# Two-layer decoder trunk on one core: the small fp32 matmuls of the state space and of the attention heads are issued in longer runs, and the last heads' transposes come one stage later

## The chip, the cores and the metric

The kernel runs on one core of a Trainium2 chip. The metric is device time in microseconds (us); of the kernel before it is the median of three runs. A core has five engines with a program each: TensorE (PE, matrix products), VectorE (DVE), ScalarE (ACT), GpSimd (POOL) and SyncE (SP, which here only starts DMAs). They meet at semaphores.

## The reference

A trunk of two layers over 256 tokens of 2048 channels, all in fp32. Layer 0 mixes tokens with a state space (Mamba-2: 64 heads of 64 channels in 8 groups), layer 1 with a forgetting attention (16 heads of 128 channels). Each layer goes on with a SwiGLU feed-forward and a per-layer embedding. Cut to what the change touches:

```python
# state space, per group of 8 heads, in 2 chunks of 128 tokens
y = ssd_chunked_scan(xs, dt, a, bm, cm) + xs * d_skip
y = y * silu(z)
yg = y.reshape(b, l, g, SSD_D_INNER // g)
yg = yg * lax.rsqrt(jnp.mean(yg * yg, axis=-1, keepdims=True) + EPS)   # one mean per group and token
mix = (yg.reshape(b, l, SSD_D_INNER) * norm_w) @ w_out

# attention, per head and block of 128 queries
s = q[lo:hi] @ k[:hi].T + csum[lo:hi, None] - csum[None, :hi]          # masked above the diagonal
o = softmax(s) @ v[:hi]
```

## The kernel before

**The stream of weights.** Almost all the work is products of the 256 tokens with weights. SP streams the weights from HBM in blocks of 512 KB (`raw`). ACT casts a block to the reduced type fp32r (`wh`, line 182) and DVE subtracts to get the part that was lost (`wl`, line 187). Activations are kept in two parts as well. So a product of a 128 x 128 weight block is two matmuls on PE: `wh` with both parts of the activations, 512 columns (line 249), and `wl` with the high part, 256 columns (line 251). Both kinds are exact to fp32 together. A `unit` (line 202) takes a column block of the weights and runs through its rows in stages of one weight block each, into 4 PSUM accumulators `acc` (6 in the last units of a layer's part); the pool `psa` has six banks for them. PSUM's two other banks are the tile `mi` of `misc()` (line 272), for everything small.

**The tasks in between.** After each stage, `unit` takes a task from the queue `bg` (lines 254 to 256) and emits it. A `noop` in the queue moves what follows by a stage. So the order of the lists of tasks sets in which stage a small piece of work stands. A scheduler that walks through the program with modelled durations then puts the instructions of all engines in their final order; `joined` (line 312) tells it that the rest of a run of matmuls may be issued only after the first of them, so that the run comes in one piece where the scheduler sees its data ready. With `hold` the order of the program is kept as well, and the next stage follows the run.

**State space.** For a group g the tasks of `core_tasks` (line 946) compute the decays on ACT (`decay`, `decay2`), transpose the group's x (`xpose`, line 961) and multiply: `ymm` (line 1008) issues 16 fp32 matmuls whose outputs have 64 partitions. They come as eight pairs (s = 0, 1), the two of a pair on different halves of PE's columns; in four of the pairs each matmul has 256 columns, in the four others 128. `y_of` (line 1012) adds the skip term on DVE. The gate's unit (`z_unit`, line 1093) multiplies y by silu(z), squares it (`sumsq`, lines 297 to 301: ACT squares, DVE adds to the tile `gss`), and then come three tasks of `gate_tasks` (line 1028): `gn1` sums `gss` over its partitions with two matmuls of one column with `ones` (`rstd_small`, line 331) and takes the root on POOL, `gn2` spreads it (`rstd_wide`, line 347), `gn3` scales y. The tile `gss` has one buffer, so that the next group's first square waits until the sums are done.

**Attention.** The four quads of heads come from `quad_tasks` (line 1258): `scores` of two heads (four matmuls, line 1267, then DVE and the exponentials on ACT), `norm` (line 1287, a division on DVE), `turns` (six 128 x 128 transposes, line 1299, then two copies `pT` on ACT, line 1306) and `values` (eight matmuls, line 1315). The last quad stands under the output projection, whose stages are six accumulators wide and take 12 matmuls each; before that projection's column 12 the queue is drained (`need`, line 1348), which sets where the last `values` stand.

Of the kernel before, what the change touches and what calls it, by code (L numbers as in the profile page):

```python
# [7 lines left out]
F32 = mybir.dt.float32  # L8
# [6 lines left out]
P = 128  # L15
T = 256
# [5 lines left out]
NG = 8  # L22
# [34 lines left out]
def tile_trunk(ctx, tc, a, out):  # L57
# [214 lines left out]
    def misc():  # L272
        return psm.tile([P, 512], F32, tag="mi", name=nm("mi"))
# [51 lines left out]
        turn.append(last_v[0])  # L325
        return r

    def rstd_small(acc, n):
        ps = misc()
        for j in range(2):  # L330
            PE.matmul(ps[:, j:j + 1], lhsT=acc[:, j * P:(j + 1) * P], rhs=ones[:, :1],
                      start=True, stop=True)
        ms = tmp("ms", (P, 2))
        dmark[0] = V.tensor_scalar(out=ms, in0=ps[:, :2], scalar1=1.0 / n, scalar2=EPS,  # L334
                                   op0=mult, op1=add)
        rs = tmp("rs", (P, 2), bufs=3)
        G.tensor_tensor(out=rs, in0=ms, in1=mhalf, op=ALU.pow)  # L337
        return rs
# [464 lines left out]
    with ExitStack() as ys:  # L803
        yp = pool(ys, "yp", side="right")
        y = [yp.tile([P, T], F32, name=f"y{c}") for c in range(32)]
        with ExitStack() as st:
# [136 lines left out]

            s3 = [None]

            def core_tasks(g, xg):
                S = {}
                for q in range(2):
                    h0 = 8 * g + 4 * q
                    ab = s3[0].tile([P, 4, T], F32, tag="ab", name=nm("ab"), bufs=2)  # L950
                    G.dma_start(
                        out=ab.rearrange("p a n -> p (a n)"),
                        in_=acd[h0:h0 + 4, :].rearrange("h n -> (h n)").partition_broadcast(P))
                    S[f"a{q}"] = ab

# [51 lines left out]

                def ymm():
                    todo = ymm_of(1) + ymm_of(0)
                    joined(todo[0], todo[1:])  # L1010

                def y_of(q):
                    for pr in range(2):
# [6 lines left out]
                def ymm_y():  # L1020
                    ymm()
                    y_of(1)

                return [lambda: decay(0, 0), lambda: decay(0, 1), xpose, lambda: decay2(0),
                        lambda: decay(1, 0), lambda: decay(1, 1), lambda: decay2(1), noop, ymm_y,
                        lambda: y_of(0), noop]

            def gate_tasks(g, S):
                def gn1():
                    S["rs"] = rstd_small(S["ss"], 512)  # L1030

                def gn2():
                    S["rw"] = yp.tile([P, T], F32, tag="grw", name=nm("grw"), bufs=1)
                    rstd_wide(S["rs"], S["rw"])

                def gn3():
                    for c in range(4):
                        yc = y[4 * g + c]
                        last_v[0] = V.scalar_tensor_tensor(out=yc, in0=yc, scalar=col("ssd_norm", 4 * g + c),
                                               in1=S["rw"], op0=mult, op1=mult)  # L1040
                if g < NG - 2:
                    return [noop, gn1, gn2, gn3]
                late.append(lambda: paced(gn3))
                return [noop, gn1, gn2] if g < NG - 1 else [gn1, noop, gn2, noop]

# [45 lines left out]
            left = [0]  # L1091

            def z_unit(g, pops):
                S = {}

                def ev_z(t, acc):
                    if t == 0:
                        while len(bg) > left[0]:
                            bg.popleft()()
                    if t == 0:  # L1100
                        S["ss"] = yp.tile([P, T], F32, tag="gss", name=nm("gss"), bufs=1)
                        if g == 0:
                            gated(0, z00)
                    if g == 0:
                        t += 1
                    yc = y[4 * g + t]
                    if g == NG - 1:
                        later.append((acc, yc, S["ss"]))
                        return
                    z = tmp("g0")  # L1110
                    gather(acc, z)
                    gated(t, z)

                def gated(t, z):
                    yc = y[4 * g + t]
                    V.tensor_tensor(out=z, in0=z, in1=rwide2, op=mult)
                    th = tmp("th")
                    A.activation(th, z, AF.Tanh)
                    V.scalar_tensor_tensor(out=z, in0=th, scalar=1.0, in1=z, op0=add, op1=mult)
                    V.tensor_tensor(out=yc, in0=yc, in1=z, op=mult)  # L1120
                    sumsq(S["ss"], yc, t == 0)
                unit(lambda k: xs0[k], ev_z, pops=pops)
                if g < NG - 1:
                    bg.extend(gate_tasks(g, S))
                else:
                    last7.extend([late[0]] + gate_tasks(g, S) + [late[1]])
# [127 lines left out]
    ots = [newx() for _ in range(FH)]  # L1254

    RNG = ((0, P), (P, 384))

    def quad_tasks(hds, q, k):
        ck = load_ck(hds[0] // 4)
        S = [{} for _ in hds]  # L1260

        def scores(j0):
            pss = [misc(), misc()]

            def mm(i, b):
                qT, kT = q[j0 + i], k[j0 + i]
                return PE.matmul(pss[i][:, RNG[b][0]:RNG[b][1]], lhsT=qT[:, b * P:(b + 1) * P],  # L1267
                                 rhs=kT[:, :(b + 1) * P], start=True, stop=True)
            joined(lambda: mm(1, 0), [lambda i=i, b=b: mm(i, b)
                                      for i, b in ((1, 1), (0, 0), (0, 1))])  # L1270
            for i in (1, 0):
                hd, ps = hds[j0 + i], pss[i]
                sc = fp.tile([P, 384], F32, tag="sc", name=nm("sc"), bufs=4)
# [13 lines left out]
        def norm(j0):  # L1287
            for i in (1, 0):
                sc, sm = S[j0 + i]["sc"], S[j0 + i]["sm"]
                V.reciprocal(out=sm, in_=sm)  # L1290
                for j, (b, e) in enumerate(RNG):
                    V.tensor_scalar(out=sc[:, b:e], in0=sc[:, b:e], scalar1=sm[:, j:j + 1],
                                    scalar2=None, op0=mult)

        def turns(j0):
            pss = [misc(), misc()]

            def turned(i, b):
                return PE.transpose(out=pss[i][:, b * P:(b + 1) * P],
                                    in_=S[j0 + i]["sc"][:, b * P:(b + 1) * P], identity=ident)  # L1300
            joined(lambda: turned(0, 2), [lambda i=i, b=b: turned(i, b) for i in range(2)
                                          for b in range(3) if (i, b) != (0, 2)],
                   hds[-1] == FH - 1)
            for i in range(2):
                pT = fp.tile([P, 384], F32, tag="pT", name=nm("pT"), bufs=4)
                A.copy(out=pT, in_=pss[i][:, :384])
                S[j0 + i]["pT"] = pT

        def values():
            pss = [misc(), misc()]  # L1310

            def mm(i, b):
# [1 line left out]
                o = pss[i // 2][:, (i % 2) * T:(i % 2 + 1) * T]  # L1314
                return PE.matmul(o[:, b * P:], lhsT=vt[:, b, hd * P:(hd + 1) * P],  # L1315
                                 rhs=S[i]["pT"][:, b * T:(T, 384)[b]], start=b == 0, stop=b == 1)
            joined(lambda: mm(3, 0), [lambda i=i, b=b: mm(i, b)
                                      for i, b in ((3, 1), (2, 0), (2, 1), (1, 0), (1, 1), (0, 0), (0, 1))],
                   hds[-1] == FH - 1)
            for i in range(4):  # L1320
                split(pss[i // 2][:, (i % 2) * T:(i % 2 + 1) * T], ots[hds[i]])

        if hds[-1] == FH - 1:
            return [noop, lambda: scores(0), lambda: scores(2), lambda: norm(0), noop,
                    lambda: (turns(0), norm(2)), noop, lambda: turns(2), noop, values]
        return [noop, lambda: scores(0), noop, lambda: scores(2), lambda: norm(0), noop,
                lambda: (turns(0), norm(2)), noop, lambda: turns(2), noop, values]

    for u in range(4):
        q = [fp.tile([P, T], F32, tag="qk", name=nm("q"), bufs=12) for _ in range(4)]  # L1330
# [104 lines left out]
```

## Time and profile before

| what | value |
|---|---|
| time, median of 3 runs | 2753.42 us (2752.81 to 2754.73) |
| the profiled execution's own time | 2754.77 us |
| its span | 2753.0 us |
| PE busy | 2745.7 us |
| DVE busy | 1906.7 us |
| ACT busy | 1481.1 us |
| mean traffic from and to HBM | 188 GB/s |
| mean granted clock of PE | 1.0 |

The span is the time from the first to the last instruction of the profiled execution; 1.8 us of its own time lie around it. An engine's busy time is the union of its instructions' times. Matmuls follow each other in a pipeline and their ends are modelled, so that the printed duration of one matmul is longer than the distance to the next: distances between starts tell what a matmul costs.

### The profile page before, as it was taken

To read this page: it belongs to the slowest core of one execution; us is meant where nothing else is said; L and a number is where in the kernel's file an instruction comes from. 1 tells how busy PE (TensorE), PEld (TensorE's weight loads), DVE (VectorE), ACT (ScalarE), POOL (GpSimd) and SP (SyncE) were. 2 spreads that over 40 slices of the span, in tenths; PEclk is the share of its full clock that TensorE was granted. 3 is DMA by queue.
4 is the path that set the end of the run, shared out by engine and by line. 5 is a ranking of instruction groups with operands and counts; after the bars stand their busy time and mean duration, and the time that the engine had idled before them with its cause. 6 is when DMAs were issued, how large, how long until landed. Compare 5 with 4: busy or idle time off the path is not lost.

```text
span 2753.0 us, 43127 instructions
## 1 busy us (share of the span) xinstructions
PE 2745.7 (100%) x16340; PEld 2436.2 (88%) x16340; DVE 1906.7 (69%) x3146; ACT 1481.1 (54%) x2456; POOL 48.6 (2%) x104
## 2 busy tenths in 40 slices
PE   9999999999999999999999999999999999999999
PEld 8888888889888888888898998889888888888898
DVE  8888888754976645666568656766876545666577
ACT  6577677554655444444446544545654444445454
POOL 0000000000000000000000000000000000000000
PEclk9999999999999999999999999999999999999999
DMA  7666666565666656666556676655666556656555
GB/s 262 179 205 190 187 198 188 158 209 168 189 202 191 190 189 189 191 174 200 193 162 196 188 220 181 178 158 165 196 205 187 188 193 187 195 169 203 196 163 167
DMA packets 262656, 519.58 MB, mean 189 GB/s; under 512 B 17408, under 2 KB 44192, under 8 KB 262448
## 3 DMA queue, kind: packets, MB, share of 16 engines
q1 hardware_dynamic: 258784, 504.54, 59.6%
q0 software_dynamic: 3520, 12.15, 1.4%
q8 instruction: 128, 2.10, 0.3%
q14 instruction: 80, 0.66, 0.1%
q10 hardware_dynamic: 144, 0.14, 0.0%
HBM read 514.58 MB, written 2.18 MB: 188 GB/s over the span
## 4 chain that ended last, share of the span: by engine, by line
PE 98%; DVE 1%; ACT 0%; issue 0%; DMA 0%; DVEq 0%; ACTq 0%
PE acc L249 58%; PE acc L251 30%; PE acc L245 1%; PE acc L244 1%; PE acc L246 1%; PE acc L238 1%; PE acc L239 1%; PE acc L240 1%; PE mi L1002 1%; PE mi L1267 0%; PE mi L1315 0%; PE mi L347 0%; PE mi L961 0%; DVE wl L187 0%; DVE ssb L301 0%
## 5 line engine op out<-in xcount | busy, mean ns | idle before, releaser
L249 PE MATMUL acc<-x,wh 128*128 128x512 f32 x4992 | 1698.3, 393 | 0.9 <-ACT wh L182 0.5
L187 DVE TENSOR_TENSOR wl<-raw,wh 128x1024 fp32r<-128x1024 f32 (+4 forms) x1020 | 1169.8, 1152 | 725.1 <-ACT wh L182 723.3
L182 ACT CAST wh<-raw 128x1024 fp32r<-128x1024 f32 (+4 forms) x1020 | 1004.6, 991 | 967.5 <-PE acc L249 844.4
L251 PE MATMUL acc<-x,wl 128*128 128x256 f32 x4992 | 1317.3, 280 | 0.1
L249 PEld LDWEIGHTS acc<-x,wh 128*128 128x128 f32 x4992 | 923.4, 188 | 190.5 <-issue 1.4
L251 PEld LDWEIGHTS acc<-x,wl 128*128 128x128 f32 x4992 | 924.1, 188 | 25.5 <-issue 2.2
L249 PE MATMUL acc<-a,wh 128*128 128x512 f32 x1232 | 425.5, 391 | 0.0
L251 PE MATMUL acc<-a,wl 128*128 128x256 f32 x1232 | 341.9, 282 | 0.0
L249 PEld LDWEIGHTS acc<-a,wh 128*128 128x128 f32 x1232 | 229.9, 188 | 47.1
L251 PEld LDWEIGHTS acc<-a,wl 128*128 128x128 f32 x1232 | 232.6, 189 | 2.2
L249 PE MATMUL acc<-xb,wh 128*128 128x512 f32 x512 | 179.4, 393 | 0.0
L277 ACT COPY tb<-acc 128x256 f32<-128x256 f32 x400 | 140.4, 369 | 48.1 <-PE acc L251 24.7
L251 PE MATMUL acc<-xb,wl 128*128 128x256 f32 x512 | 144.9, 284 | 0.0
L249 PEld LDWEIGHTS acc<-xb,wh 128*128 128x128 f32 x512 | 95.6, 188 | 19.5
L251 PEld LDWEIGHTS acc<-xb,wl 128*128 128x128 f32 x512 | 96.7, 189 | 0.8 <-issue 0.2
L249 PE MATMUL acc<-xq,wh 128*128 128x512 f32 x224 | 77.7, 390 | 0.0
L898 DVE SCALAR_TENSOR_TENSOR g<-xr,vec,g 128x256 f32<-128x256 f32 x144 | 63.5, 479 | 11.6 <-ACT g L895 11.3
L278 DVE TENSOR_TENSOR g<-acc,tb 128x256 f32<-128x256 f32 x171 | 65.2, 417 | 0.5
L251 PE MATMUL acc<-xq,wl 128*128 128x256 f32 x224 | 63.0, 282 | 0.0
L982 ACT ACTIVATE E<-ab,bias 128x128 f32<-128x128 f32 x192 | 59.9, 391 | 1.2 <-DMA ab<-acd 1.2
L301 DVE TENSOR_TENSOR ssb<-ssb,sq 128x256 f32<-128x256 f32 x120 | 50.5, 421 | 12.0 <-ACT sq L300 8.2
L337 POOL TENSOR_TENSOR rs<-ms,mhalf 128x2 f32<-128x2 f32 x18 | 22.6, 1255 | 1993.4 <-DVE ms L334 1993.4
(228 smaller groups left out, 2158.0 us busy)
## 6 DMA issues: line engine op xcount, KB each, us to landing
raw<-down SPq DMA_DIRECT2D x176, 512.0 KB, 4.1
raw<-ssd_in SPq DMA_DIRECT2D x144, 512.0 KB, 4.5
raw<-gate SPq DMA_DIRECT2D x128, 512.0 KB, 4.2
raw<-up SPq DMA_DIRECT2D x128, 512.0 KB, 4.4
raw<-fox_in SPq DMA_DIRECT2D x64, 512.0 KB, 4.1
raw<-gate SPq DMA_DIRECT2D x64, 384.0 KB, 3.3
raw<-up SPq DMA_DIRECT2D x64, 384.0 KB, 3.4
raw<-ssd_out SPq DMA_DIRECT2D x40, 512.0 KB, 3.9
```

The source lines that it names most:

```text
L182: low_a[0] = A.copy(out=wh[:, :kc * n], in_=raw[:, :kc * n])
L187: low[0] = V.tensor_tensor(out=wl[:, :kc * n], in0=raw[:, :kc * n], in1=wh.bitcast(F32)[:, :kc * n], op=sub)
L238: PE.matmul(o, lhsT=xh, rhs=wh[:, c, :], start=st, stop=False)
L239: PE.matmul(o, lhsT=xh, rhs=wl[:, c, :], start=False, stop=False)
L240: last = PE.matmul(o, lhsT=x[:, 1, t * P:(t + 1) * P], rhs=wh[:, c, :], start=False, stop=sp)
L249: PE.matmul(accs[t], lhsT=wh[:, c, t * P:(t + 1) * P], rhs=x.rearrange("p a n -> p (a n)"), start=st, stop=False)
L251: last = PE.matmul(accs[t][:, :T], lhsT=wl[:, c, t * P:(t + 1) * P], rhs=x[:, 0, :], start=False, stop=sp)
L277: i = A.copy(out=tb[:np_], in_=acc[:np_, T:2 * T])
L278: took[0] = (i, V.tensor_tensor(out=o, in0=acc[:np_, :T], in1=tb[:np_], op=add))
L301: last_v[0] = V.tensor_tensor(out=acc, in0=acc, in1=sq, op=add)
L898: V.scalar_tensor_tensor(out=c, in0=xr[:, k:k + T], scalar=col(f"conv_w{k}", cc), in1=c, op0=mult, op1=add)
L982: A.activation(E[:, i, b * P:(b + 1) * P], ab[:, i, lo:lo + P], AF.Relu, scale=-1.0, bias=bias3[:, b, h0 + i:h0 + i + 1])
```

## The change

There are three parts.

**State space.** For the groups 1 to 6, the two matmuls with `ones` that sum the squares of the group before (`sums_mm`) are put at the end of the group's run of y matmuls, and write to a tile that is taken from the accumulators' pool. The y matmuls of these groups stand four stages later in the list, and `gn2` and `gn3` of the group before follow them; groups 0 to 5 have no tasks of their own for this any more.

**Attention, quads 0 to 2.** The transposes of a quad's first two heads are put behind the scores of its other two, and the values of the quads 0 and 1 behind the first scores of the next quad (`kept`). Scores with such company take their PSUM tiles from the accumulators' pool (`spare`). Stages are spaced anew.

**Attention, last quad.** `norm(2)` stands alone; `turns(0)`, `turns(2)` and `values` come one place later in the list.

```diff
-    def rstd_small(acc, n):
-        ps = misc()
-        for j in range(2):
-            PE.matmul(ps[:, j:j + 1], lhsT=acc[:, j * P:(j + 1) * P], rhs=ones[:, :1],
-                      start=True, stop=True)
+    def sums_mm(acc, ps):
+        return [lambda j=j: PE.matmul(ps[:, j:j + 1], lhsT=acc[:, j * P:(j + 1) * P],
+                                      rhs=ones[:, :1], start=True, stop=True)
+                for j in range(2)]
+
+    def rstd_small(acc, n, ps=None):
+        if ps is None:
+            ps = misc()
+            for f in sums_mm(acc, ps):
+                f()
         ms = tmp("ms", (P, 2))
...
                 S = {}
+                with_sums = 0 < g < NG - 1
...
                     todo = ymm_of(1) + ymm_of(0)
+                    if with_sums:
+                        ss = gate_s[g - 1]["ss"]
+                        sums = psa.tile([P, 512], F32, tag="acc", name=nm("acc"))
+                        todo += sums_mm(ss, sums)
                     joined(todo[0], todo[1:])
+                    if with_sums:
+                        gate_s[g - 1]["rs"] = rstd_small(ss, 512, sums)
 
...
                     y_of(1)
 
-                return [lambda: decay(0, 0), lambda: decay(0, 1), xpose, lambda: decay2(0),
-                        lambda: decay(1, 0), lambda: decay(1, 1), lambda: decay2(1), noop, ymm_y,
-                        lambda: y_of(0), noop]
+                begin = [lambda: decay(0, 0), lambda: decay(0, 1), xpose, lambda: decay2(0),
+                         lambda: decay(1, 0), lambda: decay(1, 1), lambda: decay2(1)]
+                if not with_sums:
+                    return begin + [noop, ymm_y, lambda: y_of(0), noop]
+                return begin + [noop] * 4 + [ymm_y, lambda: y_of(0),
+                                             lambda: gate_f[g - 1][0](), lambda: gate_f[g - 1][1](),
+                                             noop]
 
...
                 if g < NG - 2:
-                    return [noop, gn1, gn2, gn3]
+                    gate_f[g] = (gn2, gn3)
+                    return []
...
+        def spare():
+            return psa.tile([P, 512], F32, tag="acc", name=nm("acc"))
+
+        def scores(j0, more=None):
+            pss = [spare(), spare()] if more else [misc(), misc()]
+            rest, end = more() if more else ([], noop)
...
-                                      for i, b in ((1, 1), (0, 0), (0, 1))])
+                                      for i, b in ((1, 1), (0, 0), (0, 1))] + rest)
+            end()
             for i in (1, 0):
                 hd, ps = hds[j0 + i], pss[i]
                 sc = fp.tile([P, 384], F32, tag="sc", name=nm("sc"), bufs=4)
...
+        def run(mms_end):
+            todo, end = mms_end
+            joined(todo[0], todo[1:], hds[-1] == FH - 1)
+            end()
+
...
         if hds[-1] == FH - 1:
             return [noop, lambda: scores(0), lambda: scores(2), lambda: norm(0), noop,
-                    lambda: (turns(0), norm(2)), noop, lambda: turns(2), noop, values]
-        return [noop, lambda: scores(0), noop, lambda: scores(2), lambda: norm(0), noop,
-                lambda: (turns(0), norm(2)), noop, lambda: turns(2), noop, values]
+                    lambda: norm(2), lambda: run(turns(0)), noop, lambda: run(turns(2)), noop,
+                    lambda: run(values())]
+        was, kept[0] = kept[0], None
+        tasks = [noop, lambda: scores(0, was), lambda: norm(0), noop, noop, noop,
+                 lambda: scores(2, lambda: turns(0)), lambda: norm(2), noop, noop, noop,
+                 lambda: run(turns(2))]
+        if hds[-1] < FH - 5:
+            kept[0] = values
+            return tasks + [noop] * 4
+        return tasks + [noop, lambda: run(values())]
```

**The y matmuls of group 1, and the sums of group 0.** The order of PE before, at the run of y matmuls of group 1 (`mi<-E,xd`; the number behind a name tells apart tiles of one name). A first pair of 256 columns stands 14 matmuls further up, so the run has two pieces:

```order
L249 MATMUL acc_2247<-x_157,wh_2369 128x512 [waits Activation_49]
L249 MATMUL acc_2248<-x_157,wh_2369 128x512
L1002 MATMUL mi_2347<-E_2193,xd_2142 64x128 [waits DVE_49]
L1002 MATMUL mi_2347<-E_2193,xd_2142 64x128
L1002 MATMUL mi_2347<-E_2193,xd_2142 64x256 x2
L1002 MATMUL mi_2347<-E_2193,xd_2142 64x128 x2
L1002 MATMUL mi_2348<-E_2093,xd_2142 64x256 [waits PE_49]
L1002 MATMUL mi_2348<-E_2093,xd_2142 64x256
L1002 MATMUL mi_2348<-E_2093,xd_2142 64x128 x2
L1002 MATMUL mi_2348<-E_2093,xd_2142 64x256 x2
L1002 MATMUL mi_2348<-E_2093,xd_2142 64x128 x2
L251 MATMUL acc_2247<-x_157,wl_2370 128x256 [waits DVE_49]
```

After the change the first pair stands 16 matmuls further up, and behind it comes a second piece:

```order
L249 MATMUL acc_2249<-x_157,wh_2349 128x512
L249 MATMUL acc_2250<-x_157,wh_2349 128x512
L1010 MATMUL mi_2413<-E_2193,xd_2142 64x128 [waits DVE_49]
L1010 MATMUL mi_2413<-E_2193,xd_2142 64x128
L1010 MATMUL mi_2413<-E_2193,xd_2142 64x256
L251 MATMUL acc_2247<-x_157,wl_2350 128x256 [waits DVE_49]
```

The third piece begins 12 matmuls further down with the other half of the 256-column pair whose first half ends this one. So the run is cut twice instead of once, and a pair is split. One weight block behind the third piece stand the sums of group 0 (`acc_2415<-ones,gss`), by themselves, ahead of the first matmul of the next unit (`acc_2524<-x_107`):

```order
L249 MATMUL acc_2250<-x_159,wh_2371 128x512
L251 MATMUL acc_2250<-x_159,wl_2372 128x256
L249 MATMUL acc_2250<-x_160,wh_2371 128x512
L251 MATMUL acc_2250<-x_160,wl_2372 128x256
L329 MATMUL acc_2415<-ones,gss_2200 128x1 [waits DVE_49]
L329 MATMUL acc_2415<-ones,gss_2200 128x1
L249 MATMUL acc_2524<-x_107,wh_2393 128x512 [waits Activation_49]
L251 MATMUL acc_2524<-x_107,wl_2394 128x256
L249 MATMUL acc_2524<-x_146,wh_2393 128x512
```

Before, they stood 39 matmuls behind that unit's first one:

```order
L251 MATMUL acc_2525<-x_149,wl_2531 128x256
L249 MATMUL acc_2525<-x_150,wh_2530 128x512
L331 MATMUL mi_2457<-ones,gss_2200 128x1 [waits DVE_49]
L331 MATMUL mi_2457<-ones,gss_2200 128x1
L251 MATMUL acc_2525<-x_150,wl_2531 128x256
L249 MATMUL acc_2526<-x_149,wh_2530 128x512
L251 MATMUL acc_2526<-x_149,wl_2531 128x256
```

So the sums have moved forward by 39 matmuls. On DVE after the change, the last addition to `gss` with what stands around it (`ms` reads the sums):

```order
L898 TENSOR_TENSOR xr_2478<-xr_2478,rwide 128x256 [waits DVE_49]
L187 TENSOR_TENSOR wl_2564<-raw_2561,wh_2563 128x1024 [waits DMAHW6_49,PE_49,Activation_49]
L301 TENSOR_TENSOR gss_2200<-gss_2200,sq_2240 128x256 [waits Activation_49]
L903 SCALAR_TENSOR_TENSOR g_242_2470<-xr_2464,vec,g_242_2470 128x256 [waits Activation_49,Pool_49]
L903 SCALAR_TENSOR_TENSOR g_246_2484<-xr_2478,vec,g_246_2484 128x256 [waits Activation_49,Pool_49]
L903 SCALAR_TENSOR_TENSOR g_242_2470<-xr_2464,vec,g_242_2470 128x256 [waits DVE_49]
L339 TENSOR_SCALAR ms_2434<-acc_2415 128x2 [waits PE_49]
```

The addition still stands behind the subtraction for a weight block that PE uses after the sums, as it does before the change.

**The y matmuls of group 2.** On PE after the change, one lone matmul of a pair, cut off by the scheduler:

```order
L249 MATMUL acc_2807<-x_153,wh_2863 128x512
L249 MATMUL acc_2808<-x_153,wh_2863 128x512
L1010 MATMUL mi_2971<-E_2747,xd_2688 64x256 [waits DVE_49]
L251 MATMUL acc_2805<-x_153,wl_2864 128x256 [waits DVE_49]
L249 MATMUL acc_2805<-x_154,wh_2863 128x512
```

The rest follows 44 rows further down, with its partner first and the sums of group 1 at the end:

```order
L1010 MATMUL mi_2971<-E_2747,xd_2688 64x256
L1010 MATMUL mi_2971<-E_2747,xd_2688 64x128 x2
L1010 MATMUL mi_2971<-E_2747,xd_2688 64x256 x2
L1010 MATMUL mi_2971<-E_2747,xd_2688 64x128 x2
L1010 MATMUL mi_2972<-E_2631,xd_2688 64x256 x2
L1010 MATMUL mi_2972<-E_2631,xd_2688 64x128 x2
L1010 MATMUL mi_2972<-E_2631,xd_2688 64x256 x2
L1010 MATMUL mi_2972<-E_2631,xd_2688 64x128 x2
L329 MATMUL acc_2973<-ones,gss_2754 128x1 [waits DVE_49,PE_49]
L329 MATMUL acc_2973<-ones,gss_2754 128x1
L249 MATMUL acc_2805<-x_159,wh_2929 128x512 [waits Activation_49]
```

Here the run has two pieces as before the change, the cut has come between the two halves of a 256-column pair, and the sums are joined to the run. The runs of the groups 3 to 6 are whole after the change, with the sums at their end; before, those of 3 and 4 were whole, and those of 5 and 6 in two pieces.

**The last heads.** On PE before, at the transposes of the last quad's first two heads (`mi<-cst,sc`):

```order
L251 MATMUL acc_18993<-x_16974,wl_19104 128x256
L249 MATMUL acc_18994<-x_16974,wh_19103 128x512
L251 MATMUL acc_18994<-x_16974,wl_19104 128x256
L1299 MATMUL mi_19161<-cst,sc_19047 128x128 [waits DVE_49]
L1299 MATMUL mi_19161<-cst,sc_19047 128x128 x2
L1299 MATMUL mi_19162<-cst,sc_19037 128x128 x3
L249 MATMUL acc_18989<-x_16975,wh_19127 128x512 [waits Activation_49]
L251 MATMUL acc_18989<-x_16975,wl_19128 128x256
```

After:

```order
L251 MATMUL acc_18993<-x_16975,wl_19128 128x256
L249 MATMUL acc_18994<-x_16975,wh_19127 128x512
L251 MATMUL acc_18994<-x_16975,wl_19128 128x256
L1329 MATMUL mi_19185<-cst,sc_19047 128x128 [waits DVE_49]
L1329 MATMUL mi_19185<-cst,sc_19047 128x128 x2
L1329 MATMUL mi_19186<-cst,sc_19037 128x128 x3
L249 MATMUL acc_18989<-x_16976,wh_19145 128x512 [waits Activation_49]
L251 MATMUL acc_18989<-x_16976,wl_19146 128x256
```

The transposes have moved behind the 12 matmuls of the weight block `wh_19127`. The last `values` keep their place among the matmuls.

## Rows read from the trace of the kernel before

**Rows 1.** The page: PE's busy time, and the shares of the engines in the chain of work that ended last.

```profile
PE 2745.7 (100%) x16340; PEld 2436.2 (88%) x16340; DVE 1906.7 (69%) x3146; ACT 1481.1 (54%) x2456; POOL 48.6 (2%) x104
...
PE 98%; DVE 1%; ACT 0%; issue 0%; DMA 0%; DVEq 0%; ACTq 0%
```

**Rows 2.** PE's waits: who waits for whom, total us, how often, longest us.

```profile
PE mi L395 <- DVE mhalf L380: 1.1, 1, 1.1
PE mi L1299 <- DVE sc L1292: 0.7, 1, 0.7
```

**Rows 3.** PE's timeline in the attention: start and busy us, engine, line, operation, tiles, x the records in a row. Two rows of transposes and their neighbours; then the scores in one piece; then the scores in two pieces. An fp32 matmul leaves two records where its output has 128 partitions and 128 columns.

```profile
1681.38 0.28 PE L251 MATMUL acc<-xb,wl 128*128 128x256 f32 x1
1681.49 0.82 PE L1299 MATMUL mi<-cst,sc 128*128 128x128 f32 x6
1682.07 0.48 PE L249 MATMUL acc<-xb,wh 128*128 128x512 f32 x1
1682.38 0.28 PE L251 MATMUL acc<-xb,wl 128*128 128x256 f32 x1
...
1665.45 0.28 PE L251 MATMUL acc<-xb,wl 128*128 128x256 f32 x1
1665.57 1.47 PE L1267 MATMUL mi<-k,q 128*128 128x128 f32 x8
...
1667.00 0.40 PE L249 MATMUL acc<-xb,wh 128*128 128x512 f32 x1
...
1671.74 0.28 PE L251 MATMUL acc<-xb,wl 128*128 128x256 f32 x1
1671.86 0.82 PE L1267 MATMUL mi<-k,q 128*128 128x128 f32 x4
...
1672.75 0.82 PE L1267 MATMUL mi<-k,q 128*128 128x128 f32 x4
...
1673.52 0.39 PE L249 MATMUL acc<-xb,wh 128*128 128x512 f32 x1
```

**Rows 4.** PE's timeline at y matmuls: a run in one piece (first four rows), a run in two pieces (next four), and two 64-column matmuls that stand alone, without a partner (last three).

```profile
338.90 0.40 PE L249 MATMUL acc<-x,wh 128*128 128x512 f32 x1
339.22 2.82 PE L1002 MATMUL mi<-E,xd 128*64 128x256 f32 x32
341.97 0.39 PE L251 MATMUL acc<-x,wl 128*128 128x256 f32 x1
342.20 0.39 PE L249 MATMUL acc<-x,wh 128*128 128x512 f32 x1
...
437.43 0.39 PE L249 MATMUL acc<-x,wh 128*128 128x512 f32 x1
437.75 0.65 PE L1002 MATMUL mi<-E,xd 128*64 128x256 f32 x4
...
438.64 2.39 PE L1002 MATMUL mi<-E,xd 128*64 128x128 f32 x28
...
441.30 0.28 PE L251 MATMUL acc<-x,wl 128*128 128x256 f32 x1
...
82.15 0.28 PE L251 MATMUL acc<-x,wl 128*128 128x256 f32 x1
82.36 0.65 PE L876 MATMUL mi<-cst,dtk 128*64 128x128 f32 x4
...
83.28 0.28 PE L251 MATMUL acc<-x,wl 128*128 128x256 f32 x1
```

**Rows 5.** The timelines of PE, ACT and DVE at the sums of group 0; a bracket tells for how long an engine was idle ahead of the row, and for whom.

```profile
206.50 0.39 PE L249 MATMUL acc<-x,wh 128*128 128x512 f32 x1
...
213.32 0.39 PE L331 MATMUL mi<-ones,gss 128*128 128x1 f32 x3
...
206.62 1.05 ACT L182 CAST wh<-raw 128x1024 fp32r<-128x1024 f32 x1 [0.87 <-ACT tb L277]
...
208.09 1.22 DVE L187 TENSOR_TENSOR wl<-raw,wh 128x1024 fp32r<-128x1024 f32 x1
209.22 0.42 DVE L301 TENSOR_TENSOR gss<-gss,sq 128x256 f32<-128x256 f32 x1
```

**Rows 6.** The timelines of ACT and DVE at a later group: its first square and its last addition to `gss`.

```profile
386.16 0.42 ACT L297 ACTIVATE gss<-y 128x256 f32<-128x256 f32 x1 [2.60 <-DVE y L1120]
...
398.05 0.42 DVE L301 TENSOR_TENSOR gss<-gss,sq 128x256 f32<-128x256 f32 x1
```

**Rows 7.** The timelines of PE, DVE and ACT at the last quad.

```profile
1827.52 0.28 PE L251 MATMUL acc<-x,wl 128*128 128x256 f32 x1
1828.50 0.88 PE L1299 MATMUL mi<-cst,sc 128*128 128x128 f32 x6 [0.70 <-DVE sc L1292]
1829.13 0.48 PE L249 MATMUL acc<-x,wh 128*128 128x512 f32 x1
...
1827.90 0.55 DVE L1292 TENSOR_SCALAR sc<-sc,sm 128x128 f32<-128x128 f32 x2
...
1834.25 0.86 ACT L1306 COPY pT<-mi 128x384 f32<-128x384 f32 x2
```

**Rows 8.** PE's timeline at the start of the program.

```profile
5.76 2.50 PE L249 MATMUL acc<-x,wh 128*128 128x512 f32 x5 [0.50 <-ACT wh L182]
...
9.13 1.33 PE L249 MATMUL acc<-x,wh 128*128 128x512 f32 x4
```

More of the change, by code (lines that the diff above doesn't have):

```diff
@@ L944, in tile_trunk @@
             s3 = [None]
+            gate_s, gate_f = {}, {}
             def core_tasks(g, xg):
                 S = {}
+                with_sums = 0 < g < NG - 1
                 for q in range(2):
@@ L1093, in z_unit @@
             def z_unit(g, pops):
-                S = {}
+                S = gate_s[g] = {}
                 def ev_z(t, acc):
@@ L1256, in tile_trunk @@
     RNG = ((0, P), (P, 384))
+    kept = [None]
     def quad_tasks(hds, q, k):
@@ L1260, in quad_tasks @@
         S = [{} for _ in hds]
-        def scores(j0):
-            pss = [misc(), misc()]
+        def spare():
[3 more added lines that the diff above has]
+            rest, end = more() if more else ([], noop)
             def mm(i, b):
@@ L1300, in turned, with end @@
                                     in_=S[j0 + i]["sc"][:, b * P:(b + 1) * P], identity=ident)
[L1301 to L1307, printed above, removed]
+            def end():
+                for i in range(2):
+                    pT = fp.tile([P, 384], F32, tag="pT", name=nm("pT"), bufs=4)
+                    A.copy(out=pT, in_=pss[i][:, :384])
+                    S[j0 + i]["pT"] = pT
+            return [lambda i=i, b=b: turned(i, b) for i, b in
+                    ((0, 2), (0, 0), (0, 1), (1, 0), (1, 1), (1, 2))], end
         def values():
@@ L1316, in mm, with end @@
                                  rhs=S[i]["pT"][:, b * T:(T, 384)[b]], start=b == 0, stop=b == 1)
[L1317 to L1321, printed above, removed]
+            def end():
+                for i in range(4):
+                    split(pss[i // 2][:, (i % 2) * T:(i % 2 + 1) * T], ots[hds[i]])
+            return [lambda i=i, b=b: mm(i, b) for i in (3, 2, 1, 0) for b in range(2)], end
         if hds[-1] == FH - 1:
             return [noop, lambda: scores(0), lambda: scores(2), lambda: norm(0), noop,
-                    lambda: (turns(0), norm(2)), noop, lambda: turns(2), noop, values]
-        return [noop, lambda: scores(0), noop, lambda: scores(2), lambda: norm(0), noop,
-                lambda: (turns(0), norm(2)), noop, lambda: turns(2), noop, values]
+                    lambda: norm(2), lambda: run(turns(0)), noop, lambda: run(turns(2)), noop,
[8 more added lines that the diff above has]
+        return tasks + [noop, lambda: run(values())]
     for u in range(4):
```

## The prediction

> **What bounds the kernel now.** I read the page first. PE is busy in 2745.7 of 2753.0 us and makes 98% of the chain that ended last [rows 1]. So the time is PE's time, and an edit counts only by what it does to the distances between PE's starts. The second view is the list of PE's waits: the two longest are 1.1 us at the start and 0.70 us at the transposes of the last quad's first heads [rows 2]; there is hardly any idle time to win. The third is PE's timeline. There the starts are to be read, not the printed durations. A pair of matmuls for one weight block, 512 and 256 columns, takes 0.35 us from start to start at the normal pace (0.23 and 0.12), and what a small run costs is the distance around it less the matmuls between.
>
> **What a longer run saves.** The six transposes of a normal quad: from the 256-column matmul ahead (1681.38) to the one behind (1682.38) it is 1.00 us, less the pair's 0.35 leaves 0.65 us, which is 0.11 for each of the six records and next to nothing for the change from one kind to the other [rows 3]. The scores show the same directly. In one piece they take 1667.00 − 1665.45 = 1.55 us with two 256-column matmuls in it, so 1.31 us. In two pieces it is 1.78 us with two 256-column and one 512-column matmul in it, so again 1.31 us [rows 3]. A cut between matmuls with all 128 columns of PE in use is free within 0.02 us. It is another thing with the y matmuls, whose outputs have 64 columns. A whole run takes 342.20 − 338.90 − 0.35 = 2.95 us; a run with one cut, 441.30 − 437.43 less a pair and one 512-column matmul more (0.35 + 0.23), takes 3.29 us [rows 4]. So a cut there costs 0.34 us.
>
> Two 64-column matmuls without a partner, of 128 columns each, take 83.28 − 82.15 − 0.35 = 0.78 us [rows 4]. Less 0.34 us for the start and end of such a run, that is 0.22 us each, one after the other. In the whole run 16 matmuls, 24 times 128 columns, would then take 5.3 us if they ran singly; they take 2.95 us, so the two of a pair run side by side. A pair of 256 columns that is split costs a second pass, 2 × 0.22 = 0.44 us; below, it could cost nothing if its late half found other work to run beside, which its neighbours (pairs that are complete) don't offer. I take 0.44.
>
> **The change, part by part.** All is against the profiled execution, 2754.77 us (2753.0 of span and 1.8 around it), 1.35 us above the median.
>
> *Joins.* Ten runs are put behind another: the sums of five groups, three sets of transposes, two of values. At 0.01 us each they give back 0.1 us. The bounds are 0 and 0.34 each, the price of a 64-column cut, which would be 3.4 us; the scores in two pieces stand nearest to what is joined and show none of it.
>
> *The y runs.* Group 1 gets one more cut, +0.34, and a split pair, +0.44. Group 2 keeps its number of pieces and gets a split pair, +0.44. Groups 5 and 6 come in one piece, −0.68. The sum is +0.54.
>
> *The sums of group 0.* This is the largest term. These sums aren't joined; they only come 39 matmuls earlier. At that place PE is at 206.50 before [rows 5], and with the 0.34 and 0.44 us that group 1's run costs more it gets there at 207.28. But what they sum is not ready. The last addition to `gss` starts on DVE at 209.22 and ends at 209.64; ahead of it in DVE's queue, in both orders, is the subtraction of a weight block (208.09, 1.22 us), which needs the cast of 206.62 (1.05 us) on ACT [rows 5]. That cast writes into a buffer that PE's last stage before this place frees, so it can't begin much before PE gets there. Before, PE ran on for 39 matmuls, to 213.32, and the addition was long done. Now PE waits. If nothing on ACT and DVE shifts, it waits from 207.28 to 209.64, 2.4 us. If all of it shifts with PE by the 0.78 us, 3.1 us. I take the middle, 2.8 us, since part of the chain hangs on DVE's and ACT's own work, and 2.0 to 3.6 for the range. Behind the waiting sums on PE stands all of the next unit; the weights that pile up meanwhile help nobody, for PE hardly waits for any later.
>
> *The sums of groups 1 to 5.* They stand behind the y run of the group after, about seven stages behind the products that they need. From a later group's first square (386.16) to its last addition (398.05 + 0.42) are 12.3 us [rows 6]; seven stages of 8 pairs at 0.35 are 19.6 us. The 7 us left cover a subtraction or two in DVE's queue. I take no wait. The next group's first square, which needs the buffer, and the scaling of y come later, and nobody reads y before the output projection.
>
> *Attention, quads 0 to 2.* The matmuls are the same, and there is no wait at them now but for the one of the last quad [rows 2]. Scores that borrow two of the six accumulators, of which a unit holds four, could keep the next unit's first matmul waiting until DVE has read them. I take nothing, since a score tile is read within the same stage or the next; a wait of the size of the one seen, 0.70, in three quads would be 2.1 us.
>
> *Last quad.* The transposes wait for the division, which ends at 1827.90 + 0.55 = 1828.45 [rows 7]. They cost 1829.13 − 1827.52 less 0.12, and 0.08 more behind them: 1.57 us against the normal 0.65, so 0.92 us to win. After, 12 matmuls (six pairs, 2.1 us) come first, and PE arrives at 1829.7, 1.2 us behind the division. What is late next could be the values: they keep their place, so they stand 12 matmuls behind the second transposes instead of 24, and the two copies (0.86 us [rows 7]) and a cast must be done by then. With 0.65 us of transposes and 2.1 us of matmuls in between, and 0.86 + 0.83 (taken as a cast of this size) of ACT work after the first transposes, some 1.1 us are spare. −0.92.
>
> The sum: +2.8 + 0.54 − 0.92 − 0.1 = **+2.3 us**, 2757.1 for the profiled execution, and 2753.4 + 2.3 = 2755.7 us for the median.
>
> **Rivals.** *The clock falls.* PE would be idle for 2.8 us at the sums of group 0. The longest wait inside the trace is the 0.70 us at 1828.50, and behind it the six transposes still take 0.63 us, the full pace [rows 7]. At the start, after which PE is at half its pace, five pairs take 9.13 − 5.76 = 3.37 us, 0.67 each against 0.35 [rows 8], which is the level of 1.2 GHz against 2.4. PE's first work there follows the wait of 1.1 us [rows 2], so the low level lasts some 8.5 us, until about 9.6. If the wait brings that back once, it costs 8.5 × (1 − 0.35/0.67) = 4.1 us on top, and the time is 2759.8 us: slower. It decides as soon as the wait is long enough; nothing in the trace between 0.7 and 2.8 us says where that is. Against it: the engine is fully busy on both sides. The Trainium skill ("TensorE: Matmul & The Clock Gate", section "HAM oscillation — how this bites in real kernels") holds that a gap between bursts of matmuls can bring the throttled clock back, and that the following burst then starts cold; the trace has no gap long enough to confirm or refute it, and the sum does without it.
>
> *The sums aren't late.* Should the addition get ahead of the subtraction, or its input be done sooner since the gate's DVE work lies differently, the wait goes and what is left is −0.5 us: 2752.9. The order of DVE, with the addition behind the subtraction, speaks against it.
>
> *The joins save a fixed cost after all*, at up to 0.34 us each instead of 0.01. Ten of them give 3.3 us more than taken, 2752.4 us with the wait. The scores in two pieces speak against it [rows 3].
>
> *Waits for borrowed accumulators*, 2.1 us: 2757.8. It lies within the range.
>
> **How the numbers follow.** The forecast as summed has a chance of 0.68, with a range of its own of 2754 to 2757.5 (the wait from 2.0 to 3.6, the split pairs from nothing to 0.44 each). The sums not late 0.14; joins that save 0.07; the clock 0.11. A difference of 0.2%, 5.5 us, is about what a measurement of this kernel can tell from no change. The forecast, at +0.08%, and both rivals on the low side lie within it. Only the fallen clock, at 6.4 us more, gets beyond, and about three quarters of its chance do: slower 0.08. Faster by 5.5 us needs more than all the gains listed: 0.03, a half of which is for what I have not thought of. The range, 2752.3 to 2759.3, takes in the cases on the low side and part of the clock's.
>
> **What would show it.** In the profile after, the list of waits should have a row of 2 to 3.6 us at the sums of group 0, for DVE's addition to `gss`, and no longer the 0.70 us at the last transposes. The distances around the y runs should be 2.95 us for groups 3 to 6 plus 0.44 for the four records of the sums, at 0.11, and more for 1 and 2. Rows of 512 columns at 0.23 us behind the wait say that the clock stayed; 0.43 that it fell. The forecast is wrong if that wait is under 1 us, if waits appear at the values or at the first matmul of a unit behind borrowed tiles, or if joined transposes take less than 0.6 us.

## The result and the profile after

The changed kernel takes 2757.23 us (median of 22 executions, 2755.10 to 2759.07), the kernel before 2753.16 us in the same comparison: a ratio of 1.0014 [1.0008, 1.002], 4.1 us more. That is within 0.2%, and above the forecast of 2755.7 us by 1.5 us.

PE's waits after the change (who waits for whom, total us, how often, longest us):

```profile
PE acc L329 <- DVE gss L301: 2.7, 1, 2.7
PE mi L400 <- DVE mhalf L385: 1.1, 1, 1.1
PE acc L249 <- ACT wh L182: 0.9, 1, 0.9
```

The wait at the last heads' transposes [rows 2] is gone and one of 2.7 us at the sums of group 0 has come. PE's timeline there (start and busy us, as in rows 3):

```profile
205.40 0.28 PE L251 MATMUL acc<-x,wl 128*128 128x256 f32 x1
208.34 0.60 PE L329 MATMUL acc<-ones,gss 128*128 128x1 f32 x4 [2.66 <-DVE gss L301]
208.81 0.55 PE L249 MATMUL acc<-x,wh 128*128 128x512 f32 x1
209.16 0.41 PE L251 MATMUL acc<-x,wl 128*128 128x256 f32 x1
209.37 0.63 PE L249 MATMUL acc<-x,wh 128*128 128x512 f32 x1
209.80 0.41 PE L251 MATMUL acc<-x,wl 128*128 128x256 f32 x1
210.01 0.63 PE L249 MATMUL acc<-x,wh 128*128 128x512 f32 x1
...
212.54 0.40 PE L249 MATMUL acc<-x,wh 128*128 128x512 f32 x1
...
212.89 0.39 PE L249 MATMUL acc<-x,wh 128*128 128x512 f32 x1
```

A pair takes 0.35 us ahead of the wait; behind it a pair takes 0.64 (209.37 to 210.01), near the pace of the program's start [rows 8], and from 212.5 on 0.35 again. The view of stretches gives the granted clock in its column behind the five engines (PE, PEld, DVE, ACT, POOL):

```profile
207.00:209.00 2.00, 0.66 (x5) 0.66 (x6) 2.00 (x4) 1.52 (x4) 0.00 (x0) 1.00 0.03 6
209.00:212.00 3.00, 3.00 (x11) 2.54 (x11) 3.00 (x12) 0.82 (x2) 1.05 (x3) 0.51 0.58 179
...
212.40:216.00 3.60, 3.60 (x23) 3.22 (x22) 3.39 (x9) 2.26 (x4) 0.20 (x2) 0.99 0.00 0
```

So the clock fell to 1.2 GHz behind the wait: it was still granted in full until 209.0, while the sums ran, and was at half from then until about 212.5. From the start of the sums to the seventh pair behind them are 212.54 − 208.34 = 4.20 us. In the control below, with the same wait and the full clock, they are 2.64 us (208.61 to 211.25). So the low stretch, six pairs long, cost 1.6 us.

The last heads' transposes and their neighbours, to be set beside [rows 7], and joined scores and transposes, beside [rows 3]:

```profile
1832.53 0.28 PE L251 MATMUL acc<-x,wl 128*128 128x256 f32 x1
1832.65 0.82 PE L1329 MATMUL mi<-cst,sc 128*128 128x128 f32 x6
1833.22 0.48 PE L249 MATMUL acc<-x,wh 128*128 128x512 f32 x1
1833.54 0.28 PE L251 MATMUL acc<-x,wl 128*128 128x256 f32 x1
...
1683.01 0.28 PE L251 MATMUL acc<-xb,wl 128*128 128x256 f32 x1
1683.13 1.47 PE L1291 MATMUL acc<-k,q 128*128 128x128 f32 x8
1684.44 0.82 PE L1329 MATMUL mi<-cst,sc 128*128 128x128 f32 x6
1685.02 0.48 PE L249 MATMUL acc<-xb,wh 128*128 128x512 f32 x1
1685.33 0.28 PE L251 MATMUL acc<-xb,wl 128*128 128x256 f32 x1
```

The last transposes now cost 1.01 − 0.35 = 0.66 us. The joined run costs 2.32 − 0.35 = 1.97 us, as much as its two parts alone (1.31 and 0.65).

The two profiled spans, 2753.0 before and 2755.1 after, differ by less than the medians, because PE comes to its full pace at the start at another time in each execution: in the profile before after some 9.6 us [rows 8], in the one after already ahead of the first stage, as its first rows show. By 11.1 us the profile after has 15 pairs of the first stages behind it and the one before ten; the five are 1.75 us.

```profile
5.74 1.43 PE L249 MATMUL acc<-x,wh 128*128 128x512 f32 x5 [0.89 <-ACT wh L182]
7.01 0.75 PE L251 MATMUL acc<-x,wl 128*128 128x256 f32 x5
7.60 1.33 PE L249 MATMUL acc<-x,wh 128*128 128x512 f32 x5
...
9.35 1.33 PE L249 MATMUL acc<-x,wh 128*128 128x512 f32 x5
...
11.11 1.09 PE L249 MATMUL acc<-x,wh 128*128 128x512 f32 x4
```

That the clock makes this difference is read from the pace alone. The column of the granted clock shows 1.00 in both profiles, also where the one before has PE at half pace:

```profile
6.00:8.00 2.00, 2.00 (x5) 1.58 (x6) 1.92 (x4) 2.00 (x7) 0.00 (x0) 1.00 1.04 368
```

The 22 executions lie in three groups: 3 at 2755.1 to 2755.5 us with a mean clock of 1.000, 11 at 2756.6 to 2757.4 with 0.999, and 8 at 2758.5 to 2759.1 with 0.998 or 0.999.

### The profile page after: what moved, and what is told of

Its sections match the earlier page's. It is cut to its first block, busy times and chain, and to the rows that moved or that the text cites. A ratio compares the mean times of both kernels' runs of the same rounds, so it can differ in the third digit from the quotient of the medians.

```text
span 2755.1 us, 43113 instructions
## 1 busy us (share of the span) xinstructions
PE 2745.4 (100%) x16340; PEld 2436.2 (88%) x16340; DVE 1908.3 (69%) x3146; ACT 1480.5 (54%) x2456; POOL 45.9 (2%) x104
## 4 chain that ended last, share of the span: by engine, by line
PE 98%; DVE 1%; ACT 0%; issue 0%; DMA 0%; DVEq 0%; ACTq 0%
PE acc L249 58%; PE acc L251 30%; PE acc L244 1%; PE acc L246 1%; PE acc L245 1%; PE acc L238 1%; PE acc L239 1%; PE acc L240 1%; PE mi L1010 1%; PE mi L1346 0%; PE mi L352 0%; PE mi L969 0%; DVE wl L187 0%; PE acc L1291 0%; ACT wh L182 0%
## 5 line engine op out<-in xcount | busy, mean ns | idle before, releaser
L598 ACT ACTIVATE th<-sg 128x256 f32<-128x256 f32 x88 | 33.3, 419 | 43.5 <-DVE sg L596 43.4
```

The costliest lines, as they stand in the source:

```text
L598: mark[0] = A.activation(th, sg, AF.Tanh)
```

## Experiments

Theory A: the terms of the prediction are right (+2.3 us, most of it the wait at the sums of group 0), and behind the wait the clock falls in most executions, for another 1.7 us or more. Theory B: the clock counts in single executions only, and the rest of the loss lies in the small runs. Each time is a median of 11 executions beside the kernel before on the same chip; that kernel took 2753.1 to 2753.2 us on all three chips.

**The sums of group 0 pinned (control).** The sums are no longer left to the scheduler but fixed between the two units, and `gn2` and `gn3` of group 0 follow in the next unit (the new function; its call is not shown):

```diff
+            def sums0():
+                ss = gate_s[0]["ss"]
+                sums = psa.tile([P, 512], F32, tag="acc", name=nm("acc"))
+                ins = last_pe[0]
+                for f in [lambda: PE.matmul(sums[:, P:2 * P], lhsT=ones, rhs=ones, start=True, stop=True)
+                          for _ in range(FILL)] + sums_mm(ss, sums):
+                    with after(ins):
+                        ins = f()
+                pe_turn[0] = ins
+                gate_s[0]["rs"] = rstd_small(ss, 512, sums)
```

`FILL` is 0 here; `last_pe` is the last matmul of the stage before.

> The changed kernel with the sums of group 0 fixed where they stand, between two units, as the control for the next run. Theory A (the changed kernel loses 2.7 us in the wait for these sums and some 1.7 us more because the clock falls behind it in most executions; the other terms sum to -0.8 us): as the changed kernel, 2757.2 us, some executions at 2755.3, and a wait of 2.7 us at the sums in the profile with pairs at 0.64 us behind it. Theory B (the clock counts in single executions only, and the rest of the loss is in the cuts and joins of the small runs): also 2757.2 us; this run doesn't tell them apart alone.

Measured: 2756.89 us, 1.0014 [1.0005, 1.0023]. One of the 11 executions, at 2755.48 us, had a mean clock of 1.000, and it is the one that was profiled:

```profile
205.68 0.28 PE L253 MATMUL acc<-x,wl 128*128 128x256 f32 x1
208.61 0.61 PE L331 MATMUL acc<-ones,gss 128*128 128x1 f32 x4 [2.66 <-DVE gss L303]
209.08 0.48 PE L251 MATMUL acc<-x,wh 128*128 128x512 f32 x1
209.40 0.28 PE L253 MATMUL acc<-x,wl 128*128 128x256 f32 x1
209.51 0.39 PE L251 MATMUL acc<-x,wh 128*128 128x512 f32 x1
209.74 0.28 PE L253 MATMUL acc<-x,wl 128*128 128x256 f32 x1
```

The same wait of 2.66 us stands there with 0.35 us a pair behind it (209.40 to 209.74). So the wait doesn't bring the low clock every time, and where it doesn't the time is near what the sum gave, 2.4 us above the kernel before.

**The idle time filled.** `FILL = 12`.

> As the control, but PE has 12 useless 128 x 128 fp32 matmuls (0.22 us each, 2.64 us) in the place of its idle time ahead of the sums; the sums can't start earlier than in the control. Theory A: the clock stays at its full level, the pairs behind the sums come at 0.35 us, and the time falls by 1.7 us to 2755.4 us, the wait itself being still paid. Theory B: no change against the control, 2757.2 us. If the useless matmuls get in the way: above 2757.2.

Measured: 2755.26 us (2754.99 to 2755.82), 1.0008 [0.9999, 1.0017]; all 11 executions have a mean clock of 1.000. PE's timeline:

```profile
205.82 0.28 PE L253 MATMUL acc<-x,wl 128*128 128x256 f32 x1
205.94 2.84 PE L1102 MATMUL acc<-ones 128*128 128x128 f32 x24
208.75 0.61 PE L331 MATMUL acc<-ones,gss 128*128 128x1 f32 x4
209.22 0.48 PE L251 MATMUL acc<-x,wh 128*128 128x512 f32 x1
209.54 0.28 PE L253 MATMUL acc<-x,wl 128*128 128x256 f32 x1
```

The sums start no earlier than before, and PE does 2.6 us of useless work, yet the time falls by 1.6 us against the control. Theory A holds: that part of the loss is the clock's. Theory B, which left nothing for this run to win, falls.

**The sums five weight blocks later.**

```diff
-                if g == 2:
-                    sums0()
...
+                    begin[1] = lambda: (decay(0, 1), sums0())
+                    begin[2] = lambda: (xpose(), gate_f[0][0]())
+                    begin[3] = lambda: (decay2(0), gate_f[0][1]())
```

> As the control, but the sums of group 0 stand five weight blocks further down in the next unit, where what they sum has long been ready. Theory A: no wait and no fall of the clock, 2753.2 - 0.8 = 2752.4 us. Theory B: only the 2.7 us of the wait go, 2754.5 us.

Measured: 2752.31 us, 0.9997 [0.9989, 1.0006], all clocks 1.000, no wait at the sums. The control is 4.6 us above this run. The wait with the restart behind it makes 2.9 of them: by the control's rows, 209.40 − 205.68 less a pair (0.35) and less what the sums cost in this run without a wait (0.45). The low stretch in the changed kernel's profile makes 1.6.

**The attention's part alone**, on the kernel before; and of it **the last heads alone** (the edit shown):

```diff
-                    lambda: (turns(0), norm(2)), noop, lambda: turns(2), noop, values]
+                    lambda: norm(2), lambda: turns(0), noop, lambda: turns(2), noop,
+                    values]
```

> The kernel before with the attention's part of the change alone. Both theories: the wait of 0.7 us and its restart go, 0.92 us, and five joins give nothing: 2752.2 us, ratio 0.9997. If the joins save 0.34 us each: 2750.5. If borrowed accumulators or later values make PE wait: 2753.5 or more, with a row in the list of waits.

> The kernel before with the last quad's tasks alone one place later. If the gain of the attention's part is all here: -0.92 us, 2752.2 us, as the attention's part whole. If the joins of the quads 0 to 2 carry some of it: above 2752.4.

Measured: 2752.12 us, 0.9996 [0.9988, 1.0005], and 2752.30 us, 0.9997 [0.9988, 1.0006]. Both gain about the 0.92 us of the wait and its restart; the five joins in the quads 0 to 2 have given nothing that shows. The two runs were on different chips, so that 0.1 us between them says nothing.

**Shorter idle times.** `FILL = 4` and `FILL = 8`; the profiles show 1.76 and 0.87 us of idle time left.

> As the control of the first call, with 4 useless matmuls (0.9 us) in place of a part of PE's idle time, so that about 1.8 us of idle time are left ahead of the sums. Theory A (it is the length of the idle stretch that brings the low clock): fewer or shorter falls than the control, 2755.3 to 2756.5 us. If any idle time above 1 us does it: as the control, 2756.9. If 0.9 us of work ahead of the idle time is enough to keep the clock: 2755.3.

> With 8 useless matmuls (1.8 us), so that about 0.9 us of idle time are left. Theory A: no fall, near the 0.7 us of the kernel before, which showed none; 2755.3 us. If any idle time above 0.7 us does it: 2756 or more.

Measured: 2756.80 us, 1.0012 [1.0004, 1.0021], with a mean clock under 1.000 in 7 of 11; and 2755.70 us, 1.0009 [1.0000, 1.0018], with 1.000 in all. PE's rows at the sums, with 4 and with 8 useless matmuls:

```profile
208.38 0.61 PE L331 MATMUL acc<-ones,gss 128*128 128x1 f32 x4 [1.76 <-DVE gss L303]
...
210.48 0.61 PE L331 MATMUL acc<-ones,gss 128*128 128x1 f32 x4 [0.87 <-DVE gss L303]
```

The second has no fall, as theory A expects. The first lies above theory A's 2755.3 to 2756.5 and at the 2756.9 of the rival by which any idle time above 1 us does it; the next run, with 1.29 us and no fall, speaks against that one. So the loss doesn't shrink evenly with the idle time. Four executions with `FILL = 8` took 2757.1 to 2757.7 us; the one of them that was profiled came late to its full pace at the start, as in [rows 8].

**Square and addition ahead of the weight block.** On the control:

```diff
+        if i == 75:
+            lag[0].append(first75[0])
+            turn.append(first75[1])
```

`first75` holds group 0's last square (ACT) and addition (DVE); the cast and subtraction of the block are issued behind them.

> As the control of the first call, but the cast and the subtraction of the one weight block that stood ahead of group 0's last square and addition are put behind these. If the prediction's reading is right that this block's work makes the wait as long as it is: the square can start at 206.3 behind a copy, the addition at 206.8, and the wait falls from 2.7 to about 1.5 us; 1.2 us less than the control without a fall of the clock (2754.1), and with falls in some executions 2754.1 to 2755.7. If the wait is set by the gate's own chain (y, its square): still 2.7 us.

Measured: 2754.58 us, 1.0003 [0.9994, 1.0012], a wait of 1.29 us, and all clocks at 1.000. PE's row at the sums; then DVE's timeline, the addition, and behind it the subtraction, which stood ahead of it in [rows 5].

```profile
207.56 0.61 PE L334 MATMUL acc<-ones,gss 128*128 128x1 f32 x4 [1.29 <-DVE gss L306]
...
206.42 0.75 DVE L903 TENSOR_TENSOR xr<-xr,rwide 128x256 f32<-128x256 f32 x2
207.08 0.42 DVE L306 TENSOR_TENSOR gss<-gss,sq 128x256 f32<-128x256 f32 x1
207.58 1.22 DVE L192 TENSOR_TENSOR wl<-raw,wh 128x1024 fp32r<-128x1024 f32 x1
```

Half of the wait was this block's work in the queues. The other half was not taken apart: the gate's own chain stands in it, and so do two multiplications of other work on DVE (206.42), directly ahead of the addition.

**A longer wait.** Two multiplications by one ahead of the addition.

```diff
+            for _ in range(more):
+                V.tensor_scalar(out=sq, in0=sq, scalar1=1.0, scalar2=None, op0=mult)
             last_v[0] = V.tensor_tensor(out=acc, in0=acc, in1=sq, op=add)
```

> As the control, with two more multiplications by one on DVE ahead of group 0's last addition, which with three instructions that come between make the wait about 1.7 us longer, 4.3 us. Theory A with the loss growing with the length of the idle time: falls in all executions, 2757 (without a fall) + 1.7 or more: 2758.6 to 2760. If the fall costs the same whatever the length: 2758.6. If the clock has nothing to do with the idle time: 2756.9 + 1.7 = 2758.6 with pairs at 0.35 us behind the wait.

Measured: 2759.50 us (2758.64 to 2761.89), 1.0023 [1.0014, 1.0032], with a mean clock under 1.000 in all 11. The wait was 4.33 us. The timeline of the profiled one, at 2759.73 us:

```profile
209.87 1.01 PE L333 MATMUL acc<-ones,gss 128*128 128x1 f32 x4 [4.33 <-DVE gss L305]
...
216.01 0.63 PE L251 MATMUL acc<-x,wh 128*128 128x512 f32 x1
216.44 0.36 PE L253 MATMUL acc<-x,wl 128*128 128x256 f32 x1
216.64 0.39 PE L251 MATMUL acc<-x,wh 128*128 128x512 f32 x1
```

The low clock lasts until 216.5, nine pairs instead of six. With a full clock this kernel would take 2755.3 + 1.7 = 2757.0 us; the median is 2.5 us above that. By distances the low stretch of the profiled execution cost 3.1 us, from the sums to the tenth pair behind them 216.64 − 209.87 = 6.77 us against the control's 3.68 (208.61 to 212.29). So the loss does grow with the wait.

**The changed kernel again**, as the control of these two.

> The changed kernel once more, on the chip of these two runs, as their control: 2757.2 us, executions at 2755.3 where the clock stays and at 2757 where it falls; its profile shows one or the other.

Measured: 2756.81 us, 1.0013 [1.0004, 1.0022]; 2 of 11 at 2755.3 to 2755.4 us with a mean clock of 1.000, the others at 2756.6 us or more.

**Whole runs and no wait.** The kernel with the later sums, with group 1's y run where it was before the change, and group 2's held together:

```diff
-                    return begin + [noop] * 4 + [ymm_y, lambda: y_of(0), noop, noop, noop]
+                    return begin + [noop, ymm_y, lambda: y_of(0)] + [noop] * 6
...
-                    joined(todo[0], todo[1:])
+                    with after(last_pe[0] if g == 2 else None):
+                        joined(todo[0], todo[1:], g == 2)
```

> The control with the sums of group 0 five weight blocks later, the y run of group 1 put back where it was in the kernel before (one cut) and the y run of group 2 held in one piece. Against the run with the sums later (2752.3 us): group 1 gives back 0.74 us (4.09 us for its three pieces against 3.34 for two), group 2 gives 0.77 us (4.17 for two pieces with the sums against 3.40): 2750.8 us. If a held run makes PE wait for its data: more, with a row in the list of waits.

Measured: 2751.29 us (2750.81 to 2753.33), 0.9993 [0.9984, 1.0001]: 1.0 us under the run with the later sums where 1.5 were expected. In its profile both runs are in the shape that was expected and no new wait stands, so where the other 0.5 us are is not settled. Its median is the lowest of all, 1.8 us under the kernel before and 5.9 under the changed one; the interval against the kernel before just reaches 1, so that a gain over it is not shown.

## Why the prediction came out as it did

The time lies in the range and in the forecast's own range, and the side is right, but a part of it came from a rival that was given 0.11. That it lies in the forecast's own range is luck: the terms named there (a wait of 3.6 us at most, the split pairs at most at the 0.44 already taken) reach 2755.7 + 0.8 = 2756.5 us, and the upper end was put at 2757.5. Without the fall the changed kernel takes 2755.3 us, near the forecast's 2755.7.

The sum was right, term by term, as far as it went. The wait at the sums of group 0 was put at 2.8 us and is 2.66 (2.9 with the restart). Moving the block's work away took half of it, so that part of its cause was read rightly. The split of group 2, forecast at 0.44 us, is seen in PE's timeline after the change: one matmul of a pair by itself, and later the rest of the run with the sums.

```profile
245.32 0.86 PE L249 MATMUL acc<-x,wh 128*128 128x512 f32 x3
246.11 0.65 PE L1010 MATMUL mi<-E,xd 128*64 128x256 f32 x2
246.69 0.39 PE L251 MATMUL acc<-x,wl 128*128 128x256 f32 x1
246.92 0.39 PE L249 MATMUL acc<-x,wh 128*128 128x512 f32 x1
...
254.10 0.28 PE L251 MATMUL acc<-x,wl 128*128 128x256 f32 x1
254.31 2.81 PE L1010 MATMUL mi<-E,xd 128*64 128x256 f32 x30
257.05 0.61 PE L329 MATMUL acc<-ones,gss 128*128 128x1 f32 x4
257.52 0.48 PE L249 MATMUL acc<-x,wh 128*128 128x512 f32 x1
257.83 0.28 PE L251 MATMUL acc<-x,wl 128*128 128x256 f32 x1
```

The first piece is two records (one matmul) and takes 0.65 us, as long as the four records of a pair in [rows 4]; by distances it costs 246.92 − 245.32 less three matmuls of 0.23 and one of 0.12, 0.79 us. The second costs 257.83 − 254.10 − 0.35 = 3.38 us, 2.94 without the sums, as much as a whole run though a matmul is missing. Together 3.73 us against 3.29 for a clean cut: 0.44. In the same way group 1's three pieces cost 4.07 us against 3.32 for its two before, 0.75 for the forecast's 0.78. Groups 5 and 6, in one piece, gave the 0.68 us; the last transposes cost 0.66 us against 1.57, −0.91 for −0.92; the joins gave nothing, for 0.1. The measured terms sum to +2.3 us (2.5 with the restart). Executions in which the clock stayed, at 2755.3 us, are 2.1 to 2.2 us above the kernel before.

What failed is the step on the clock. The prediction gave the rival 2759.8 us at a chance of 0.11, arguing that the longest wait in the trace, 0.70 us, left the pace as it was and that PE is fully busy on both sides. It happened in 19 of 22 executions. The price was wrong as well: I had taken the 8.5 us at the start of the program as the length of the low stretch, for 4.1 us, though the granted clock shows 1.00 there and only the pace is that of the low level. It is six pairs and 1.6 us in the profiled execution. With the price that this shows the rival would have stood at 2757.3 us, beside the measured 2757.2. A wait of 2.8 us was four times the longest that the trace had shown harmless, so that the row bore out nothing for it, and the chance should have been near one half.

The Trainium skill's rule ("TensorE: Matmul & The Clock Gate", section "HAM oscillation — how this bites in real kernels"), that a gap between bursts can bring back the throttled clock and the next burst starts cold, is what the trace now shows, with 0.64 us a pair against 0.35. It differs in one thing: behind the wait of 2.66 us PE did not start cold, for the sums ran at the full clock and the fall came at 209.0, 0.7 us after PE went on. Behind the wait of 4.33 us the sums were slow already, 1.01 us of busy time against 0.61.

Still open is what the third group of executions (2758.5 us and more) is. It would fit a low stretch of twice the length, as behind the longer wait, or a fall together with a late rise of the pace at the start, which is worth 1.75 us. The mean clock hints that both occur: it is 0.998 in five of the eight, as in the profiled execution behind the longer wait, and 0.999 in three, as in the middle group. No execution of that group was profiled.

## What to carry to other kernels

Where PE is the bound, moving a matmul ahead of its data costs the wait and can cost what the clock loses behind it, here 2.66 and 1.6 us; price both, and let an order in which PE never runs dry stand before one that saves a few tenths at a cut. Joining full-width fp32 matmuls into longer runs saved nothing here; for runs with 64-column outputs a cut cost 0.34 us and a split pair 0.44, and these are to be looked for in the order of instructions, since a scheduler may move them. Where single executions differ by more than the effect, look at each execution's clock before explaining a median.

## What the runs showed that was not expected

The share of executions with a fall of the clock went with the idle time at this one place: none of 11 each at 0.87 and at 1.29 us, 7 of 11 at 1.76, 38 of 44 at 2.66 (the changed kernel twice and the control), all 11 at 4.33. The two shares in the middle are too near each other to be told apart with so few executions. Useless matmuls in the idle time were worth 1.6 us. And PE comes to its full pace at the start at different times in executions of one kernel, for up to 1.75 us, without a trace in the granted clock.
